# Depthwise-convolution taps on TensorE in units of 512 prompt columns, and both layer norms behind the last unit

## The chip, the cores and the metric

The kernel runs on one core of a Trainium2 chip (TensorE is PE, VectorE is DVE, ScalarE is ACT, GpSimd is POOL, SyncE is SP). The metric is the time of one execution on the device, in microseconds (us). The kernel before takes 1607.35 us, the median of three runs (1606.72 to 1612.57).

## What is computed

One inference step of a decoder of two layers, each a token mixer and a SwiGLU feed-forward, for 512 prompt tokens and 64 sample tokens (8 sequences of 8) with a model width of 1024. The first layer's mixer is a causal convolution module, and the change is inside it; the second layer's is stick-breaking attention over a paged cache. All data are fp32; a large product is made of three products of rounded parts.

```python
def conformer_conv(h, prefix, w_pw1, b_pw1, w_dw, b_dw, ln_g, ln_b, w_pw2, b_pw2):
    u = h @ w_pw1 + b_pw1
    a, gate = jnp.split(u, 2, axis=-1)
    u = a * jax.nn.sigmoid(gate)
    u_ext = jnp.concatenate([prefix.astype(u.dtype), u], axis=1)
    c = lax.conv_general_dilated(u_ext, w_dw[:, None, :], ..., feature_group_count=D_MODEL) + b_dw
    c = jax.nn.silu(layernorm(c, ln_g, ln_b))
    return c @ w_pw2 + b_pw2, u_ext[:, -CONV_STATE:]
```

The convolution has 31 taps for each of the 1024 channels, and the layer norm is over the channels of each token.

## The kernel before, in words

Channels lie on the partitions, in 8 tiles `t` of 128; the 576 tokens (512 of the prompt, 64 of the samples) are columns, in two halves `h` of 288 columns (`HALF`). The first half holds 288 prompt tokens; the second the other 224 and the 64 sample tokens.

The whole convolution stage is one graph of operations (`conv_graph`). Each operation names its engine, an estimated cost, and what it reads and writes by name; `run_ops` plays the graph through, always gives a free engine the ready operation with the longest remaining path, and so fixes the order of the instructions on each engine. On the chip every engine follows its order and waits for its data.

The stages are:

1. The first projection (`gemm`, line 580): for each `t` two products of 48 matmuls, whose results become a gate on ACT and a product on DVE (`glu_gate`, `glu_up`). DVE also does all 31 taps of the sample columns (`sample_mul`, `sample_sum`, `sample_close`, lines 661 to 679, in two pieces of 16 and 15 taps) and the last three of the 31 taps of the prompt columns (`dve_taps`, line 649). POOL and PE write out the convolution state (`state`), through two `flat` buffers.
2. The taps on PE: 28 of the 31 taps of the prompt columns. A unit is one half of the tokens of one channel tile, 16 units in all (first all tiles of half 0, then all of half 1; loop at line 864). DVE builds the unit's 28 diagonals of 32x32 (`diag`, line 615). `taps` (line 621) issues 112 matmuls of 32x32, each on one of the array's 16 places: partitions 32i of the input by a quarter 32j of the output, where the four `j` take four different taps. The trace has two records for each of these fp32 matmuls. The unit fills four PSUM banks, one for each `i`; ACT and DVE copy two each to SBUF (`tap_copy`, line 633), four matmuls add up the four quarters (`tap_sum`, line 636), and DVE adds that to its own taps (`tap_add`, line 646).
3. The layer norm of a half: `ln_first` (line 789) gets the mean by PE (`ln_mean_pe`, from a sum over six tiles that POOL made and the last two tiles), subtracts it on DVE and squares on ACT. For half 0 POOL adds the squares of the tiles and one set of token sums on PE finishes them; for half 1 PE does a set for every tile (`token_sums`, line 698). `ln_second` (line 814) takes the variance, the power on POOL, a broadcast on PE (`ln_bc`), the multiplication on DVE, silu and the rounded high part on ACT, and the low part on DVE. The norm of half 0 is put into the graph at units 8 and 11 and so runs beside the taps of half 1; the norm of half 1 comes behind the last unit, beside the second projection of half 0.
4. The second projection (`pw2`, line 833): six channel tiles of half 0, then two of half 1, 24 matmuls each; the rest belongs to the feed-forward's own graph (`ffn`, line 914), which begins with `mix_mm` for the tiles left.

PSUM has eight banks, in two sets of four. `take(s)` deals the banks of set `s` out in turn; unit `n` uses set `n % 2`. The squares have four buffers (`sq4`), dealt out in turn in program order.

Of the kernel before, what the change touches and what calls it, by code (L numbers as in the profile page):

```python
# [16 lines left out]
P = 128  # L17
D = 1024
# [43 lines left out]
def hybrid_step_kernel(  # L62
# [494 lines left out]
    with phase:  # L557
# [15 lines left out]
        csum, rstd = rbc, sacc  # L573
# [3 lines left out]

        NP = (HALF, TP - HALF)

# [53 lines left out]
        def tap_copy(c, i, b, n):  # L633
            (nc.scalar.copy, nc.vector.tensor_copy)[i % 2](cps[c][:, i, 0:n], banks[b][:, 0:n])

        def tap_sum(c, b, n):
            for i in range(4):
                r = slice(32 * i, 32 * i + 32)
                nc.tensor.matmul(
                    banks[b][r, 0:n], ident4, cps[c][:, i, 0:n], start=True, stop=True, tile_position=(0, 32 * i)  # L640
                )

        def c_part(t, h):
            return c_sb[:, t, h * HALF : h * HALF + NP[h]]

        def tap_add(t, h, b):
            nc.vector.tensor_add(c_part(t, h), c_part(t, h), banks[b][:, 0 : NP[h]])

        def dve_taps(t, h):
            c = c_part(t, h)  # L650
            for k in range(PET, W):
                u = ups[t][:, h * HALF + k : h * HALF + k + NP[h]]
# [5 lines left out]
        spr = cv.tile([P, 16, TS], F32, name="spr")  # L658
        reds = [cv.tile([P, TS], F32, name=f"red{r}") for r in range(2)]

        def sample_mul(t, r):
            k0, k1 = ((0, 16), (16, W))[r]
            u0 = us[:, t, k0, 0:1]
            win = bass.AP(tensor=us.tensor, offset=u0.offset, ap=[u0.ap[0], [NB, k1 - k0], [1, TS]])
            nc.vector.tensor_mul(
                spr[:, 0 : k1 - k0, :], win,
                vec[:, t, R_DW + k0 : R_DW + k1, None].to_broadcast([P, k1 - k0, TS]),
            )

        def sample_sum(r):  # L670
            nc.vector.tensor_reduce(
                reds[r], spr[:, 0 : 16 - r, :].rearrange("p k c -> p c k"), axis=mybir.AxisListType.X, op=ALU.add
            )

        def sample_close(t):
            nc.vector.scalar_tensor_tensor(
# [81 lines left out]
        def conv_graph():  # L758
# [13 lines left out]
            def state(t):  # L772
                f, b = ring("flat", 2), take(t % 2)
# [6 lines left out]
            def reduce_(n):  # L780
                h, t = divmod(n, NT)
                c, b = n % 2, take(n % 2)
                do("P", 0.55, [f"cp{c}_{i}" for i in range(4)], [f"b{b}"], tap_sum, c, b, NP[h])
                do("D", 0.34, [f"b{b}"] + [f"cs{t}"] * h, [f"c{t}_{h}"], tap_add, t, h, b)
                if 0 < t < SUMS:
                    cs = csum[:, HS[h]]
                    do("G", 0.76, [f"c{t}_{h}", f"c0_{h}"], [f"sum{h}"], add, cs, c_sb[:, 0, HS[h]] if t == 1 else cs, c_sb[:, t, HS[h]])

            def ln_first(h, s):
# [8 lines left out]
                qs = rstd[:, HS[h]]  # L798
                if h:
                    b = take(s)  # L800
                    do("D", 0.1, [], [f"b{b}"], nc.vector.memset, banks[b][:, 0:3], 0.0)
                for t in range(NT):
                    if t == 0 and h == 0:
                        do("A", 0.34, [f"c{t}_{h}"], ["qs"], ln_square, qs, t, h)
                        continue
# [8 lines left out]
            def ln_second(h, s, b=None):  # L814
                if h == 0:
                    b = take(s)
                    do("D", 0.1, [], [f"b{b}"], nc.vector.memset, banks[b][:, 0:3], 0.0)
                    do("P", 0.5, ["qs"], [f"b{b}"], token_sums, h, rstd[:, HS[h]], b, True, True)
# [5 lines left out]
                if h == 0:  # L824
                    do("A", 0.34, [name], ["qs"], nc.scalar.copy, rstd[:, HS[h]], m)
                    m, name = rstd[:, HS[h]], "qs"
# [15 lines left out]
            for t in range(NT):  # L842
# [12 lines left out]
                for r in range(2):  # L855
                    do("D", 1.1, [f"u{t}_1"], ["spr"], sample_mul, t, r)
                    do("D", 1.13, ["spr"], [f"red{r}"], sample_sum, r)
                do("D", 0.2, ["red0", "red1"], [f"cs{t}"], sample_close, t)
# [4 lines left out]
            stats = None  # L863
            for n in range(2 * NT):
                h, t = divmod(n, NT)
                d, c = ring("dg", 2), n % 2
                do("D", 1.1, [], [f"dg{d}"], diag, t, d)
                bs = [take(n % 2) for _ in range(4)]
                for m0, m1 in ((0, 4), (4, PET // 4)):
                    do(  # L870
                        "P", 0.6 * (m1 - m0), [f"dg{d}", f"u{t}_0"] + [f"u{t}_1"] * h, [f"b{b}" for b in bs],
                        taps, t, h, d, bs, m0, m1,
                    )
                do("D", 0.4 * (W - PET), [f"u{t}_0"] + [f"u{t}_1"] * h, [f"c{t}_{h}"], dve_taps, t, h)
                for i, b in enumerate(bs):
                    do("AD"[i % 2], 0.36, [f"b{b}"], [f"cp{c}_{i}"], tap_copy, c, i, b, NP[h])
                if n:
                    reduce_(n - 1)
# [1170 lines left out]
```

## Time and profile before

| | |
|---|---|
| median of three runs | 1607.35 us (1606.72 to 1612.57) |
| the profiled execution | 1609.35 us, of which its span from the first to the last instruction is 1607.6 us |
| PE busy | 1510.4 us, 94% |
| DVE, ACT, POOL busy | 1248.0 us (78%), 782.3 us (49%), 407.2 us (25%) |
| first projection until | 133.9 us |
| taps on PE | 133.9 to 240.4 us |
| second projection in the convolution's graph | 241.2 to 279.4 us |

The profile is of one execution, and its times count from its first instruction. A busy engine executes an instruction; PE's matmuls overlap, so that their durations add up to more than the time they take, and starts have to be compared. "issue" names idle time for which the profile shows no other engine or transfer to wait for. PEclk is the granted share of TensorE's clock.

### The profile page before, as it was taken

What the parts mean: (1) busy time and instruction counts of PE and PEld (TensorE: products, weight loads), DVE (VectorE), ACT (ScalarE), POOL (GpSimd) and SP (SyncE); (2) the same over time, 40 slices, a digit from 0 to 9 for tenths busy, and PEclk for the clock granted to TensorE, in tenths of its full rate; (3) what the DMA queues carried; (4) which work ended last, traced back from release to release, by engine and by line L of the source; (5) the groups of instructions that cost most, each with busy time, mean ns of one, the idle gap of its engine ahead of it and who ended that gap; (6) DMA issues with size and microseconds to landing.
All of it is one profiled execution on the core that took longest, in us unless ns stands there. A gap on an engine that the chain in (4) does not pass through costs nothing. (4 is left out here: it accounts for less than half of the span.)

```text
span 1607.6 us, 35925 instructions
## 1 busy us (share of the span) xinstructions
PE 1510.4 (94%) x14371; PEld 1352.6 (84%) x14371; DVE 1248.0 (78%) x2155; ACT 782.3 (49%) x1665; POOL 407.2 (25%) x410
## 2 busy tenths in 40 slices
PE   7999989899999999999999988999998999999997
PEld 7996559889999999987988875555797999999997
DVE  5998544699989999982689985555459998999884
ACT  5223123355546545552667664444435554654553
POOL 3110211333323322350244450000132322332210
PEclk9999998999999999999999989999999999999999
DMA  6233001023222233233321227999612222232231
GB/s 184 76 88 87 4 5 38 29 80 92 93 92 89 85 103 93 70 89 95 91 68 43 73 81 293 407 406 398 217 37 66 92 93 94 90 93 93 92 101 64
DMA packets 152047, 180.23 MB, mean 112 GB/s; under 512 B 6106, under 2 KB 130530, under 8 KB 151864
## 3 DMA queue, kind: packets, MB, share of 16 engines
q1 hardware_dynamic: 151448, 176.36, 33.2%
q8 instruction: 113, 1.85, 0.5%
q10 hardware_dynamic: 432, 1.57, 0.3%
q14 instruction: 54, 0.44, 0.1%
HBM read 170.45 MB, written 8.18 MB: 111 GB/s over the span
## 5 line engine op out<-in xcount | busy, mean ns | idle before, releaser
L953 DVE TENSOR_TENSOR wlo<-fs,whi 128x512 fp32r<-128x512 f32 (+1 forms) x256 | 233.5, 913 | 26.8 <-ACT whi L135 18.8
L1095 PE MATMUL fb<-ahi,whi 128*128 128x288 f32 x704 | 210.7, 299 | 14.2 <-ACT ft L135 9.4
L135 ACT CAST whi<-fs 128x512 fp32r<-128x512 f32 (+1 forms) x256 | 157.1, 614 | 134.9 <-PE fb L1095 115.6
L1095 PE MATMUL fb<-xe,whi 128*128 128x288 f32 x1056 | 216.1, 297 | 0.1
L1095 PE MATMUL fb<-alo,whi 128*128 128x288 f32 x704 | 207.7, 295 | 7.9 <-DVE alo L953 7.9
L1095 PE MATMUL fb<-ahi,wlo 128*128 128x288 f32 x704 | 211.1, 300 | 2.3 <-DVE wlo L953 2.3
L1095 PEld LDWEIGHTS fb<-xe,whi 128*128 128x128 f32 x1056 | 170.4, 189 | 0.5 <-issue 0.3
L1095 PE MATMUL fb<-xe,wlo 128*128 128x288 f32 x528 | 159.1, 301 | 2.7 <-DVE wlo L953 2.6
L1095 PEld LDWEIGHTS fb<-ahi,whi 128*128 128x128 f32 x704 | 133.3, 189 | 17.9 <-ACT ft L135 12.4
L1095 PEld LDWEIGHTS fb<-alo,whi 128*128 128x128 f32 x704 | 134.4, 191 | 8.8 <-DVE alo L953 8.8
L1095 PEld LDWEIGHTS fb<-ahi,wlo 128*128 128x128 f32 x704 | 133.2, 189 | 5.0 <-DVE wlo L953 5.0
L953 DVE TENSOR_TENSOR wlo<-wraw,whi 128x512 fp32r<-128x512 f32 (+1 forms) x160 | 124.0, 782 | 5.7 <-ACT whi L135 5.2
L135 ACT CAST whi<-wraw 128x512 fp32r<-128x512 f32 (+1 forms) x160 | 98.0, 613 | 51.8 <-PE fb L1095 46.0
L1095 PEld LDWEIGHTS fb<-xe,wlo 128*128 128x128 f32 x528 | 99.6, 189 | 7.5 <-DVE wlo L953 7.1
L135 POOL TENSOR_TENSOR fs<-wraw 128x512 f32<-128x512 f32 (+1 forms) x32 | 47.1, 1473 | 210.5 <-DVE wlo L953 210.5
L223 ACT CAST whi<-wraw 128x1024 fp32r<-128x1024 f32 (+1 forms) x43 | 44.9, 1044 | 110.7 <-PE cb L585 48.3
L135 POOL TENSOR_TENSOR fs<-wraw,fs 128x512 f32<-128x512 f32 (+1 forms) x64 | 86.0, 1343 | 50.5 <-DVE wlo L953 44.2
L135 POOL TENSOR_TENSOR fs<-fr 128x512 f32<-128x512 f32 (+1 forms) x32 | 43.7, 1364 | 208.3 <-DVE wlo L953 208.3
L1095 PE MATMUL fb<-he,whi 128*128 128x288 f32 x456 | 93.0, 297 | 2.1 <-DVE x L135 2.0
L628 PE MATMUL cb<-up,dg 32*32 32x288 f32 (+1 forms) x3584 | 80.6, 385 | 13.8 <-issue 13.5
L1095 PE MATMUL fb<-bhi,whi 128*128 128x288 f32 x304 | 90.3, 297 | 2.1 <-DVE x L135 2.1
L1095 PE MATMUL fb<-bhi,wlo 128*128 128x288 f32 x304 | 90.1, 296 | 0.0
(375 smaller groups left out, 4078.1 us busy)
## 6 DMA issues: line engine op xcount, KB each, us to landing
kr<-in_cache_k_dram SPq DMA_DIRECT2D x64, 512.0 KB
vr<-in_cache_v_dram SPq DMA_DIRECT2D x64, 512.0 KB
wraw<-in_ffn_w_up_dram SPq DMA_DIRECT2D x44, 512.0 KB
wraw<-in_cv_w_pw_dram SPq DMA_DIRECT2D x24, 512.0 KB
wraw<-in_ffn_w_down_dram SPq DMA_DIRECT2D x24, 512.0 KB
wraw<-in_sb_w_qkv_dram SPq DMA_DIRECT2D x23, 512.0 KB
fr<-in_ffn_w_gate_dram SPq DMA_DIRECT2D x22, 512.0 KB
wraw<-in_ffn_w_gate_dram SPq DMA_DIRECT2D x22, 512.0 KB
```

What stands on the lines that cost most here:

```text
L135: ops[i][3](*(a() if callable(a) else a for a in ops[i][4]))
L223: nc.scalar.copy(hi[:, :n], raw[:, :n])
L628: nc.tensor.matmul(banks[bs[i]][rj, 0:n], dgs[d][ri, k, :], ups[t][ri, h * HALF + k : h * HALF + k + n], start=(m == 0), stop=(k >= PET - ...
L953: nc.vector.tensor_sub(dst, a, b.bitcast(F32))
L1095: nc.tensor.matmul(banks[b][:, :HALF], w[:, k, :], r[:, k, :], start=(first and k == 0 and j == 0), stop=(k == nk - 1 and j == 2), skip_gr ...
```

## The change

A unit of the taps is now all 512 prompt columns of one channel tile: eight units in place of sixteen, each with the same 112 matmuls, four copies, four summing matmuls and one add, on 512 columns. `cps` grows with it, and one `flat` buffer goes; the sample taps are done in three pieces of 10, 10 and 11 with a third small sum, added at the end. DVE's own three taps and its add go over 512 columns. The layer norms of both halves now come behind the last unit: the two `ln_first` one after the other in the graph, each in the way that only half 1 had (means used from PSUM, squares to PE's token sums for every tile), then both `ln_second`. The first two tiles of the second projection of half 0 are given to the list in steps of one `k`, and its part of half 1 takes bank set 1.

```diff
-        cps = [cv.tile([P, 4, HALF], F32, name=f"cp{i}") for i in range(2)]
-        flats = [cv.tile([P, TS + PRE], F32, name=f"flat{i}") for i in range(2)]
+        cps = [cv.tile([P, 4, TP], F32, name=f"cp{i}") for i in range(2)]
+        flats = [cv.tile([P, TS + PRE], F32, name=f"flat{i}") for i in range(1)]
...
-        def taps(t, h, d, bs, m0, m1):
-            n = NP[h]
+        def taps(t, d, bs, m0, m1):
...
-                            banks[bs[i]][rj, 0:n], dgs[d][ri, k, :], ups[t][ri, h * HALF + k : h * HALF + k + n],
+                            banks[bs[i]][rj, :], dgs[d][ri, k, :], ups[t][ri, k : k + TP],
                             start=(m == 0), stop=(k >= PET - 4), tile_position=(32 * i, 32 * j),
...
-            k0, k1 = ((0, 16), (16, W))[r]
+            k0, k1 = ((0, 10), (10, 20), (20, W))[r]
...
         def sample_close(t):
+            nc.vector.tensor_add(reds[0], reds[0], reds[2])
...
-            def reduce_(n):
-                h, t = divmod(n, NT)
-                c, b = n % 2, take(n % 2)
-                do("P", 0.55, [f"cp{c}_{i}" for i in range(4)], [f"b{b}"], tap_sum, c, b, NP[h])
-                do("D", 0.34, [f"b{b}"] + [f"cs{t}"] * h, [f"c{t}_{h}"], tap_add, t, h, b)
...
+            def reduce_(t):
+                c, b = t % 2, take(t % 2)
+                both = [f"c{t}_{h}" for h in range(2)]
+                do("P", 0.95, [f"cp{c}_{i}" for i in range(4)], [f"b{b}"], tap_sum, c, b)
+                do("D", 0.6, [f"b{b}", f"cs{t}"], both, tap_add, t, b)
...
             def ln_first(h, s):
...
-                if h == 0:
-                    do("A", 0.34, [name], [f"sum{h}"], nc.scalar.copy, csum[:, HS[h]], m)
-                    m, name = csum[:, HS[h]], f"sum{h}"
...
-                    if h == 0:
-                        do("G", 0.76, [f"sq{i}"], ["qs"], add, qs, qs, sq4[i])
-                    else:
-                        do("P", 0.5, [f"sq{i}"], [f"b{b}"], token_sums, h, sq4[i], b, t == 0, t == NT - 1)
+                    do("P", 0.5, [f"sq{i}"], [f"b{b}"], token_sums, h, sq4[i], b, t == 0, t == NT - 1)
...
-            for n in range(2 * NT):
-                h, t = divmod(n, NT)
-                d, c = ring("dg", 2), n % 2
+            for t in range(NT):
+                d, c, both = ring("dg", 2), t % 2, [f"u{t}_0", f"u{t}_1"]
                 do("D", 1.1, [], [f"dg{d}"], diag, t, d)
...
-                if n == NT:
-                    ln_first(0, 1)
-                if n == NT + 3:
-                    ln_second(0, 0)
-            reduce_(2 * NT - 1)
-            b = ln_first(1, 1)
-            ln_second(1, 1, b)
+                    do("AD"[i % 2], 0.55, [f"b{b}"], [f"cp{c}_{i}"], tap_copy, c, i, b)
+                if t:
+                    reduce_(t - 1)
+            reduce_(NT - 1)
+            first = [ln_first(h, h) for h in range(2)]
+            for h in range(2):
+                ln_second(h, h, first[h])
             for t in range(6):
-                pw2((t,), 0, 0)
-            pw2((0, 1), 1, 0, 1)
+                pw2((t,), 0, 0, 1 if t < 2 else NT)
+            pw2((0, 1), 1, 1, 1)
```

## Rows read from the trace of the kernel before

**Rows 1.** The page, part 1: busy us, share of the span, instructions.

```profile
PE 1510.4 (94%) x14371; PEld 1352.6 (84%) x14371; DVE 1248.0 (78%) x2155; ACT 782.3 (49%) x1665; POOL 407.2 (25%) x410
```

**Rows 2.** Stretches: length, busy by engine (PE, PEld, DVE, ACT, POOL), PEclk, DMA share, GB/s.

```profile
40.00:133.90 93.90, 91.86 (x690) 90.93 (x689) 87.75 (x113) 21.33 (x35) 10.98 (x25) 1.00 0.28 81
133.90:188.70 54.80, 49.11 (x1865) 29.40 (x1867) 32.88 (x52) 13.31 (x27) 5.70 (x7) 1.00 0.18 48
188.70:241.20 52.50, 43.94 (x1864) 29.35 (x1863) 28.48 (x56) 15.72 (x42) 11.80 (x13) 0.99 0.02 5
...
276.40:300.00 23.60, 23.60 (x180) 23.45 (x179) 10.09 (x18) 7.13 (x18) 11.86 (x12) 1.00 0.25 81
```

**Rows 3.** Groups by shape, PE, 133.9 to 241.2: busy, mean ns | idle before.

```profile
L628 PE MATMUL cb<-up,dg 32*32 32x288 f32 x1792 | 43.7, 411 | 5.7 <-issue 5.6
L628 PE MATMUL cb<-up,dg 32*32 32x224 f32 x1792 | 36.9, 358 | 8.1 <-issue 7.9 <-DVE c_sb L647 0.2
```

**Rows 4.** Timeline of PE: start, length of the run, instructions [idle before].

```profile
174.74 1.30 PE L639 MATMUL cb<-cp,ident 128*32 128x288 f32 x16
175.97 8.60 PE L628 MATMUL cb<-up,dg 32*32 32x288 f32 x362
...
192.78 5.71 PE L628 MATMUL cb<-up,dg 32*32 32x224 f32 x276
...
206.59 2.53 PE L628 MATMUL cb<-up,dg 32*32 32x224 f32 x128 [0.84 <-issue]
210.32 2.58 PE L628 MATMUL cb<-up,dg 32*32 32x224 f32 x124 [1.20 <-issue]
...
239.19 1.22 PE L628 MATMUL cb<-up,dg 32*32 32x224 f32 x37 [1.42 <-issue]
...
241.24 0.61 PE L744 MATMUL cb<-bhi,ahi 128*128 128x288 f32 x1
...
279.38 0.29 PE L320 MATMUL fb<-bhi,ahi 128*128 128x288 f32 x1
```

**Rows 5.** Waits, 133.9 to 241.2: us in total, times, longest.

```profile
PE cb L628 <- issue: 13.5, 15, 1.8
```

**Rows 6.** DMA queues, 133.9 to 241.2: packets, MB, share of 16 engines.

```profile
q8 instruction: 29, 0.48, 1.9%
```

**Rows 7.** Groups by shape of ACT and DVE, 136 to 241.2: tap copies.

```profile
L634 ACT COPY cp<-cb 128x288 f32<-128x288 f32 x16 | 5.9, 400 | 30.9 <-PE cb L628 17.2 <-issue 13.7
...
L634 DVE COPY cp<-cb 128x288 f32<-128x288 f32 x16 | 6.8, 453 | 21.6 <-PE cb L628 20.2 <-ACT cp L634 1.2
```

**Rows 8.** Timelines of the engines: the layer norm of the second half.

```profile
254.09 6.92 PE L702 MATMUL cb<-over_d,lsq 128*128 128x1 f32 x48
...
256.89 0.44 ACT L695 ACTIVATE lsq<-c_sb 128x288 f32<-128x288 f32 x1 [0.24 <-PE cb L702]
...
261.28 0.87 POOL L711 TENSOR_TENSOR rtok<-ln,mhalf 128x3 f32<-128x3 f32 x1 [30.93 <-DVE ln L708]
...
265.62 0.56 PE L717 MATMUL cb<-ident,rtok 96*128 96x96 f32 x3
...
266.28 2.28 DVE L723 TENSOR_TENSOR c_sb<-c_sb,cb 128x288 f32<-128x288 f32 x6
...
266.77 1.15 ACT L727 ACTIVATE c_sb<-c_sb,vec 128x288 f32<-128x288 f32 x2 [9.44 <-DVE c_sb L723]
...
268.48 0.82 DVE L733 TENSOR_TENSOR blo<-c_sb,bhi 128x288 fp32r<-128x288 f32 x2
...
268.49 1.14 ACT L727 ACTIVATE c_sb<-c_sb,vec 128x288 f32<-128x288 f32 x2
```

**Rows 9.** Stretches, as rows 2, around the token sums.

```profile
257.00:258.00 1.00, 1.00 (x9) 0.97 (x8) 0.00 (x0) 0.33 (x1) 0.00 (x0) 0.61 0.00 0
...
263.00:264.00 1.00, 1.00 (x6) 1.00 (x6) 0.00 (x0) 0.00 (x0) 0.00 (x0) 0.50 0.00 0
```

**Rows 10.** Waits of the load queue, 150 to 300 us: total, times, longest.

```profile
SPq L1083 <- DVE blo L733: 120.4, 1, 120.4
```

More of the change, by code (lines that the diff above doesn't have):

```diff
@@ L628, in taps, with tap_copy, tap_sum, tap_add @@
                         nc.tensor.matmul(
-                            banks[bs[i]][rj, 0:n], dgs[d][ri, k, :], ups[t][ri, h * HALF + k : h * HALF + k + n],
+                            banks[bs[i]][rj, :], dgs[d][ri, k, :], ups[t][ri, k : k + TP],
                             start=(m == 0), stop=(k >= PET - 4), tile_position=(32 * i, 32 * j),
                         )
-        def tap_copy(c, i, b, n):
-            (nc.scalar.copy, nc.vector.tensor_copy)[i % 2](cps[c][:, i, 0:n], banks[b][:, 0:n])
-        def tap_sum(c, b, n):
+        def tap_copy(c, i, b):
+            (nc.scalar.copy, nc.vector.tensor_copy)[i % 2](cps[c][:, i, :], banks[b])
+        def tap_sum(c, b):
             for i in range(4):
                 r = slice(32 * i, 32 * i + 32)
[L639 to L650, printed above, removed]
+                nc.tensor.matmul(banks[b][r, :], ident4, cps[c][:, i, :], start=True, stop=True, tile_position=(0, 32 * i))
+        def tap_add(t, b):
+            nc.vector.tensor_add(c_sb[:, t, 0:TP], c_sb[:, t, 0:TP], banks[b])
+        def dve_taps(t):
+            c = c_sb[:, t, 0:TP]
             for k in range(PET, W):
-                u = ups[t][:, h * HALF + k : h * HALF + k + NP[h]]
+                u = ups[t][:, k : k + TP]
                 if k == PET:
@@ L656, in dve_taps @@
                     nc.vector.scalar_tensor_tensor(c, u, col(R_DW + k, t), c, ALU.mult, ALU.add)
-        spr = cv.tile([P, 16, TS], F32, name="spr")
-        reds = [cv.tile([P, TS], F32, name=f"red{r}") for r in range(2)]
+        spr = cv.tile([P, 11, TS], F32, name="spr")
+        reds = [cv.tile([P, TS], F32, name=f"red{r}") for r in range(3)]
         def sample_mul(t, r):
-            k0, k1 = ((0, 16), (16, W))[r]
+            k0, k1 = ((0, 10), (10, 20), (20, W))[r]
             u0 = us[:, t, k0, 0:1]
@@ L772, in state @@
             def state(t):
-                f, b = ring("flat", 2), take(t % 2)
+                f, b = ring("flat", 1), take(t % 2)
                 do("G", 0.6, [f"u{t}_1"], [f"flat{f}"], state_pool, t, f)
@@ L854, in conv_graph @@
                 state(t)
[L855 to L858, printed above, removed]
+                for r in range(3):
+                    do("D", 0.75, [f"u{t}_1"], ["spr"], sample_mul, t, r)
+                    do("D", 0.78, ["spr"], [f"red{r}"], sample_sum, r)
+                do("D", 0.35, ["red1", "red2"], [f"cs{t}", "red0"], sample_close, t)
             split(2 * NT + 1)
@@ L862, in conv_graph @@
                 split(c)
-            stats = None
-            for n in range(2 * NT):
-                h, t = divmod(n, NT)
-                d, c = ring("dg", 2), n % 2
+            for t in range(NT):
+                d, c, both = ring("dg", 2), t % 2, [f"u{t}_0", f"u{t}_1"]
                 do("D", 1.1, [], [f"dg{d}"], diag, t, d)
-                bs = [take(n % 2) for _ in range(4)]
+                bs = [take(t % 2) for _ in range(4)]
                 for m0, m1 in ((0, 4), (4, PET // 4)):
[L870 to L874, printed above, removed]
-                for i, b in enumerate(bs):
-                    do("AD"[i % 2], 0.36, [f"b{b}"], [f"cp{c}_{i}"], tap_copy, c, i, b, NP[h])
-                if n:
-                    reduce_(n - 1)
-                if n == NT:
-                    ln_first(0, 1)
-                if n == NT + 3:
-                    ln_second(0, 0)
-            reduce_(2 * NT - 1)
-            b = ln_first(1, 1)
-            ln_second(1, 1, b)
+                    do("P", 0.88 * (m1 - m0), [f"dg{d}", *both], [f"b{b}" for b in bs], taps, t, d, bs, m0, m1)
+                do("D", 0.6 * (W - PET), both, [f"c{t}_0", f"c{t}_1"], dve_taps, t)
+                for i, b in enumerate(bs):
+                    do("AD"[i % 2], 0.55, [f"b{b}"], [f"cp{c}_{i}"], tap_copy, c, i, b)
[3 more added lines that the diff above has]
+            first = [ln_first(h, h) for h in range(2)]
+            for h in range(2):
+                ln_second(h, h, first[h])
             for t in range(6):
-                pw2((t,), 0, 0)
-            pw2((0, 1), 1, 0, 1)
+                pw2((t,), 0, 0, 1 if t < 2 else NT)
+            pw2((0, 1), 1, 1, 1)
             run_ops()
```

29 lines of the change are left out of this document (8 added, 21 removed).

## The prediction, written before the change was run

> **What bounds the kernel now.** The page's first part comes first: PE is busy for 94% of the span [rows 1]. So the question for any edit is which PE time it takes away or lays open. The table by stretches then splits the convolution: products of the first projection until 133.9 us, taps from 133.9 to 241.2 us, then the second projection with the second half's layer norm inside it [rows 2]. In the tap stretches PE is busy 49.1 of 54.8 and 43.9 of 52.5 us while DVE, ACT and POOL are far below, so PE works alone there and what it wastes is on the path.
>
> It wastes two things. The groups of PE by shape show 1792 tap records of 288 columns and 1792 of 224: 16 units of 224 [rows 3]. The spacing inside an unbroken run (its length, less one record, over the number less one) is (8.60 - 0.41)/361 = 22.7 ns at 288 columns and (5.71 - 0.36)/275 = 19.5 ns at 224 [rows 3, 4]. That is 0.05 ns for a further column, so a large part of a record costs the same whatever its width. And there are pauses: in the timeline runs of exactly 128 records end in idle time "issue" [rows 4], 13.5 us of PE in 15 waits [rows 5]. The instruction queue moved 29 packets in these 107.3 us [rows 6], one each 3.70 us. Some 3730 matmul records with as many weight loads stand against them [rows 2], 257 instructions a packet, 128 of them matmuls. 128 records of 224 columns take 2.5 us, far less than 3.70, and a pause follows; the start of one such run to the next is 3.73 us [rows 4]. I read the stage as held by how fast instructions arrive.
>
> **The taps.** Sixteen units become eight: 1792 records of 512 columns instead of 3584. One record: 22.7 + 224 x 0.05 = 33.9 ns, a unit 224 x 33.9 = 7.6 us. Bounds: the shortest spacing, (2.53 - 0.36)/127 = 17.1 ns in a run of 128 at 224 columns [rows 3, 4], extended by the same slope to 31.5 ns, a unit 7.1 us; in proportion to columns, 22.7 x 512/288 = 40.4 ns, a unit 9.0 us. I take 33.9: the long runs contain whatever slows a run a little, and two widths fix a line.
>
> A packet's 128 records now last 128 x 33.9 = 4.34 us, more than the 3.70 us at which packets came, so I cost the pauses at nothing; if they stay, one of 13.5/15 = 0.9 us follows each of some 14.6 packets, 13 us. The Trainium skill (Runtime: NRT & Kernel Launch, Instruction fetch mechanics) holds that the next block is fetched while the present one runs and that crossing a block is mostly hidden. The rows differ: pauses stand at every 128th matmul. By the page they have another cause and need not go; that is the first rival.
>
> The tap sums: two together hold the next taps back for 1.23 us at 288 columns (174.74 to 175.97) [rows 4], 0.6 us each. One of 512 columns I take at 1.0 us (between 0.7, if records count, and 1.1, in proportion); seven lie before the last tap's end, the eighth behind it.
>
> Stage: start 133.9 + 8 x 7.6 + 7 x 1.0 + 0.7 for a state transpose and bank waits = **202.4 us** for the last tap's end, where it is now 239.19 + 1.22 = 240.41 [rows 4]. That is 38.0 us less.
>
> **Beside the taps, at nothing.** DVE builds eight diagonals fewer and runs its own three taps in 24 instructions of 512 columns instead of 48 shorter ones, which saves fixed costs; its sample work goes from two pieces to three with one small add, which adds some. The columns stay the same, so in the first stretch its 87.8 of 93.9 us [rows 2] stays about even. Were DVE pushed there, PE would wait for gate products; each unit has a whole product of slack, so I bound it at 1 us either way. One flat buffer instead of two only makes POOL's copy wait for a transpose of the tile before, a product earlier. The copies out of PSUM (400 ns for 288 columns on ACT, 453 on DVE [rows 7]) grow, in proportion to 0.71 and 0.81 us at most, four per unit on two engines, hidden under 7.6 us. No DMA is moved by itself.
>
> **The layer norm is laid open.** Now the first half's norm lies under the second half's taps. After the change nothing stands behind the taps but the norms. From the last tap (e): two copies on each engine, e + 0.9; the sum's last matmuls, e + 1.5; the add of 512 columns (taken like a copy, 453 ns at 288 [rows 7]) from e + 1.65 to 2.35; the mean product's last operand, e + 3.2, and behind it on PE the other half's mean (1.4 us by the list's own cost), e + 4.7. Subtractions and squares feed PE's token sums: 48 records in 6.92 us for one half [rows 8]. The change does both halves that way, where now one half is added on POOL and summed once. The four square buffers are dealt out in program order, so the second half's squares follow the first's, and the list puts the broadcast behind the token sums whose remaining path is longer, nearly all of them. So I count 16 tiles' sums before the first broadcast. What is a tile's price? The last square (256.89) reuses the fourth's buffer and starts as that one's sums end: (256.89 - 254.09)/4 = 0.7 us a tile. Then the granted clock fell from full to half (2.4 to 1.2 GHz), three microseconds into the token sums, and the last four tiles took (261.0 - 256.9)/4 = 1.0 us each [rows 8, 9]. After the change PE has been half idle since e, so I take 1.0: 16 us (bounds 11 and 17), until e + 20.8. Variance, power (0.87 us on POOL, of the first half hidden) and broadcast (0.56 us at full clock), e + 21.6. The first multiplication starts at 266.28, the low half of the first split at 268.48 [rows 8]; the first matmul, which needs the high half only, can start 2.2 us behind the broadcast. **The second projection starts at e + 23.8**; now it starts 241.24 - 240.41 = 0.8 us behind the last tap [rows 4]. That costs 23.0 us.
>
> **The second projection gets shorter.** Now it runs from 241.24 to 279.38 [rows 4], 38.1 us, though its 192 matmuls (8 tile halves of 24) at 23.6/180 = 0.13 us, as in the undisturbed stretch behind it [rows 2], are some 25.5: the token sums (6.9), means, broadcast, tap sum and half clock stand inside. After the change these are done before. PE then has 25.6 us, about 1.6 us for half clock at the start (it was still half three microseconds after the token sums [rows 9]), and ACT feeds one channel tile of one half (silu and split) in (268.49 - 266.77)/2 = 0.86 us [rows 8] against 0.8 us of PE work on it, which costs about 1 us: 28.2 us. That returns 9.9 us.
>
> **Sum:** -38.0 + 23.0 - 9.9 = -24.9 us. Behind it the feed-forward order is unchanged and PE is its first stretch's limit; its first weight load waits for the last split of the second half [rows 10], which comes 15 us ahead of the projection's end instead of 6, so nothing is late there. The profiled execution took 1609.35 us (span 1607.6), 2 us above the median of 1607.35; against the median the sum is 1582.5 us.
>
> **The rivals.** *Pauses stay* (13 us): 1595.5 us. For it: 29 packets and pauses agree in number, but a queue that is only late by a constant would stay so. Against it: longer unbroken runs exist at 288 columns (362 records). *Packs don't overlap:* with one record's duration grown to 411 + 224 x (411 - 358)/64 = 597 ns [rows 3] and the next sixteen waiting for these, 41 ns a record, a unit 9.2 us, +12.8 us, 1595 us. Against it: at 288 the same would be over 25 ns, and rows show 22.7. The Trainium skill (TensorE: Matmul & The Clock Gate, Measured speedup vs the span model) gives a pack's span as one matmul's duration plus 4 ns for each further tile, which at 288 columns would be 29 ns a record; the trace disagrees, packs overlap. *Both norms before any product:* the list lets ACT finish both halves first, 14 us more ahead of the projection and little regained: 1596.5 us. *Taken back later:* the feed-forward starts no earlier because its weights do not come; its load queue is idle until then [rows 10], so they should: about 1605 us. *Slower:* fewer 32x32 tiles run at once at 512 columns. Now 411/22.7 = 18 records are in flight (durations hold the pipeline too); with 12, 597/12 = 50 ns a record, 28.9 us more than forecast, 1611.4 us. It decides from 33.9 + 24.9/1.792 = 47.8 ns. Nothing in the rows shows a limit at either width. That the change is void can be excluded: half the tap instructions are gone.
>
> **Chances.** Forecast 0.63, pauses 0.14, packs 0.07, both norms 0.06, taken back 0.06, slower 0.04. A measurement tells about 0.5% (8 us) from no change: 1599.3 us is the border. The first four lie under it, with 0.02 off for two of them together: faster 0.88, same 0.08, slower 0.04. The range: short records and full-clock token sums (-4, -5 us), with shorter tap sums (-2 us), give 1571 us, the three rivals near 1596 with some of a second one 1599 us. It holds more than eight in ten by my cases; I leave the ends because the tap price rests on two widths.
>
> **What would show it.** Taps x1792 of 512 columns spaced near 34 ns, hardly any "issue" waits in 133 to 202 us, some 15 instruction packets there; last tap near 202 us; an idle or half-clock PE for 23 us, token sums of both halves in it; first projection matmul near 226 us; the first feed-forward matmul near 254 us and the same stage lengths after it. Spacings above 40 ns, a pause per 128 records, or a projection starting later than 30 us behind the taps prove the steps wrong.

## The result and the profile after

The changed kernel takes 1579.38 us, the median of four runs (1579.24 to 1581.0); the kernel before took 1607.81 us beside it (four runs, 1606.72 to 1612.57). The ratio is 0.9819, with a 95% interval of 0.9804 to 0.9833, so 28.4 us less; 24.9 us less were forecast. The profiled executions stand 1609.35 to 1581.0 us, spans 1607.6 to 1579.2 us. The stages, from the timelines of PE:

| us from the span's start | before | predicted | after |
|---|---|---|---|
| first tap | 133.88 | 133.9 | 133.08 |
| last tap's end (e) | 240.41 | 202.4 | 199.79 |
| first matmul of the second projection | 241.24 | 226.2 | 223.59 |
| first matmul of the feed-forward | 279.38 | 254.4 | 251.99 |
| end of the span | 1607.6 | | 1579.2 |

The taps end 40.6 us earlier. Of that 23 us are given back before the projection starts, 9.7 us come back inside the projection, and the feed-forward starts 27.4 us earlier. Behind it only one more microsecond is won, which single executions differ by.

The page of the changed kernel, part 1 (busy us, share of the span, instructions), answers to [rows 1]:

```profile
PE 1497.1 (95%) x12557; PEld 1344.9 (85%) x12557; DVE 1234.3 (78%) x2123; ACT 781.8 (50%) x1647; POOL 397.0 (25%) x403
```

PE's busy time fell by 13.3 us only, against 28.4 us of the span: half of the gain is idle time of PE. The stretches show where it stood (as in [rows 2]: length, busy by engine, PEclk, DMA share, GB/s):

```profile
133.00:200.00 67.00, 67.00 (x1847) 40.74 (x1849) 36.67 (x51) 16.59 (x27) 8.86 (x12) 1.00 0.13 38
...
215.00:220.00 5.00, 5.00 (x27) 4.88 (x28) 0.00 (x0) 0.89 (x2) 0.00 (x0) 0.50 0.01 2
```

In the tap stage PE is now busy for all of 67 us, where it was busy for 93 of 107 us [rows 2]. From 215 to 220 us it is "busy" too, but almost alone, at half clock, while DVE does nothing and ACT 0.89 us: these are the token sums. The timeline of PE, beside [rows 4] and [rows 8]:

```profile
138.13 11.07 PE L624 MATMUL cb<-up,dg 32*32 32x512 f32 x320
149.14 1.97 PE L635 MATMUL cb<-cp,ident 128*32 128x512 f32 x16
151.04 15.06 PE L624 MATMUL cb<-up,dg 32*32 32x512 f32 x448
...
184.73 15.06 PE L624 MATMUL cb<-up,dg 32*32 32x512 f32 x448
199.72 1.92 PE L635 MATMUL cb<-cp,ident 128*32 128x512 f32 x16
...
204.59 16.03 PE L694 MATMUL cb<-over_d,lsq 128*128 128x1 f32 x96
220.54 0.93 PE L709 MATMUL cb<-ident,rtok 128*128 128x128 f32 x3
...
223.59 0.61 PE L736 MATMUL cb<-bhi,whi 128*128 128x288 f32 x1 [0.86 <-ACT bhi L722]
...
251.99 0.40 PE L320 MATMUL fb<-bhi,ahi 128*128 128x288 f32 x1
```

Runs of 448 taps, two whole units, now stand without a break where runs of 128 ended in "issue" before. Two sums follow each pair of units. Then 96 records of token sums (both halves, 16 tiles) fill 16 us, and only behind the last of them comes the broadcast of the first half. The group by shape (133 to 252 us, which holds all taps) and the instruction queue (133.9 to 200 us), against [rows 3] and [rows 6]:

```profile
L624 PE MATMUL cb<-up,dg 32*32 32x512 f32 x1792 | 61.1, 597 | 0.0
```

```profile
q8 instruction: 14, 0.23, 1.5%
```

The 1792 records have no idle time ahead of them at all; before, 13.5 us of "issue" stood there [rows 5]. 14 packets were fetched in place of 29.

Last, the token sums. The squares on ACT show their pace, since each takes the buffer of the square four before it (timelines of ACT, then stretches as above):

```profile
206.70 0.45 ACT L687 ACTIVATE lsq<-c_sb 128x288 f32<-128x288 f32 x1 [0.24 <-PE cb L694]
207.39 0.45 ACT L687 ACTIVATE lsq<-c_sb 128x288 f32<-128x288 f32 x1 [0.24 <-PE cb L694]
...
210.50 0.44 ACT L687 ACTIVATE lsq<-c_sb 128x288 f32<-128x288 f32 x1 [0.69 <-PE cb L694]
211.63 0.44 ACT L687 ACTIVATE lsq<-c_sb 128x288 f32<-128x288 f32 x1 [0.69 <-PE cb L694]
```

```profile
206.00:207.00 1.00, 1.00 (x10) 0.97 (x10) 1.00 (x4) 0.74 (x2) 0.00 (x0) 1.00 0.00 0
207.00:208.00 1.00, 1.00 (x10) 0.96 (x9) 1.00 (x4) 0.59 (x2) 0.00 (x0) 0.79 0.00 0
208.00:209.00 1.00, 1.00 (x6) 0.98 (x6) 1.00 (x4) 0.44 (x1) 0.00 (x0) 0.50 0.00 0
```

A tile's sums take 0.69 us at the full 2.4 GHz and 1.13 us at 1.2 GHz; the granted clock falls to half inside 207 to 208 us, three microseconds into the sums, as in [rows 9].

### The profile page after: what moved, and what is told of

Same layout as the page of the kernel before. It is cut to its first block, busy times and chain, and to the rows that moved or that the text cites. A ratio compares the mean times of both kernels' runs of the same rounds, so it can differ in the third digit from the quotient of the medians.

```text
span 1579.2 us, 32209 instructions
## 1 busy us (share of the span) xinstructions
PE 1497.1 (95%) x12557; PEld 1344.9 (85%) x12557; DVE 1234.3 (78%) x2123; ACT 781.8 (50%) x1647; POOL 397.0 (25%) x403
## 3 DMA queue, kind: packets, MB, share of 16 engines
q1 hardware_dynamic: 151448, 176.36, 33.9%
## 5 line engine op out<-in xcount | busy, mean ns | idle before, releaser
L1062 PE MATMUL fb<-blo,whi 128*128 128x288 f32 x304 | 89.0, 293 | 0.4 <-DVE blo L920 0.4
```

Of the source, the lines that this page charges most:

```text
L1062: nc.tensor.matmul(banks[b][:, :HALF], w[:, k, :], r[:, k, :], start=(first and k == 0 and j == 0), stop=(k == nk - 1 and j == 2), skip_gr ...
```

## The experiments

### Fewer columns in a tap: is it the arrival of instructions that made the pauses?

Three kernels keep the changed kernel's instructions, one for one, and only let the taps on PE (with their copies, sums and adds) work on the first N of the 512 prompt columns; PE's taps of the other columns are left out.

```diff
-   banks[bs[i]][rj, :], dgs[d][ri, k, :], ups[t][ri, k : k + TP],
+   banks[bs[i]][rj, 0:N], dgs[d][ri, k, :], ups[t][ri, k : k + N],
...
-   (nc.scalar.copy, nc.vector.tensor_copy)[i % 2](cps[c][:, i, :], banks[b])
+   (nc.scalar.copy, nc.vector.tensor_copy)[i % 2](cps[c][:, i, 0:N], banks[b][:, 0:N])
```

N = 128:

> The changed kernel with the taps, their copies, sums and adds on the first 128 of the 512 prompt columns only: the other 384 columns keep DVE's three taps alone, so a part of the convolution is left out. The number of PE instructions stays. If PE is held by the arrival of its instructions (one packet of 128 matmul records with their weight loads each 3.7 us, as in the kernel before), 1792 records still need 14 packets: 52 us for the taps, last tap near 186 us, and a pause of 1.5 us or more behind every 128 records, which by themselves last 1.9 us (14.7 ns each by the line of the prediction). If a pause is a fixed 0.9 us at each 128 records: 26 + 13 + 3 us for sums, last tap near 175 us. If pauses belong to a unit (waits for its banks), 26 + 7 + 3 us, last tap near 169 us.

N = 256:

> As the one on 128 columns, with 256 columns: the second half of each unit is left out. Arrival of instructions: the same 52 us as with 128 columns, last tap near 187 us, pauses near 1.0 us (128 records last 2.7 us by 21 ns each). A fixed pause of 0.9 us: 38 + 13 + 5 us, last tap near 189 us, that is 14 us later than with 128 columns. The two runs tell it: same end means arrival, 14 us apart means columns.

N = 384, run after the other two:

> The changed kernel with PE's taps, their copies, sums and adds on the first 384 of the 512 prompt columns (the taps of the other 128 columns are left out of PE's share). Theory (a matmul record takes as long as its columns need, but 128 of them can't come faster than once in 3.45 us, as at 128 and 256 columns): a straight line through 22.7 ns at 288 and 32.4 ns at 512 columns gives 26.9 ns, 3.44 us for 128, which is just the rate at which they come; so the last tap ends at about the same 187 us as at 128 and 256 columns, and the issue waits shrink from 4.5 us (256 columns) to under 2 us. Rival (no common rate; the time follows the columns): between 256 columns (186.2) and 512 columns (199.8), the last tap ends in the middle, at 193 us.

Measured, one run each: 1570.77 us (N = 128), 1568.38 us (256), 1571.9 us (384), beside 1581.0 us of the changed kernel's own profiled run. From the first tap to the last tap's end it is 56.0, 54.1 and 58.6 us, against 66.7 us at 512. The issue waits are 9.3, 4.5, 0.3 and 0 us; those at 128 and 256 columns as the view of waits has them (us in total, times, longest):

```profile
PE cb L624 <- issue: 9.3, 10, 2.3
PE cb L624 <- issue: 4.5, 8, 0.9
```

The timelines of PE, first at 128 columns:

```profile
133.09 2.32 PE L624 MATMUL cb<-up,dg 32*32 32x128 f32 x128
...
138.00 2.11 PE L624 MATMUL cb<-up,dg 32*32 32x128 f32 x128 [0.22 <-issue]
142.00 1.53 PE L624 MATMUL cb<-up,dg 32*32 32x128 f32 x102 [1.89 <-issue]
...
169.20 2.81 PE L624 MATMUL cb<-up,dg 32*32 32x128 f32 x128 [0.92 <-issue]
```

at 256 columns:

```profile
166.33 2.75 PE L624 MATMUL cb<-up,dg 32*32 32x256 f32 x128 [0.61 <-issue]
169.79 2.80 PE L624 MATMUL cb<-up,dg 32*32 32x256 f32 x128 [0.71 <-issue]
```

and at 384:

```profile
160.44 1.83 PE L624 MATMUL cb<-up,dg 32*32 32x384 f32 x54 [0.34 <-issue]
...
164.01 12.17 PE L624 MATMUL cb<-up,dg 32*32 32x384 f32 x448
...
177.60 12.94 PE L624 MATMUL cb<-up,dg 32*32 32x384 f32 x448
```

At 256 columns the pauses are back, behind runs of exactly 128, though the units are the same eight: so it is not the number of units that took them away, but the width. The starts of such runs lie 3.46 us apart (169.79 - 166.33), of which 2.8 us are work and about 0.65 us a pause. At 224 columns, in the kernel before, it was 2.5 us of work and a start 3.73 us [rows 4] or 3.45 us (231.73 to 235.18) after the last: less work, longer pause. At 384 columns 128 records take 3.3 to 3.6 us ((12.17 - 0.49)/447 x 128 in the run at 164.01), and one pause of 0.34 us is left; at 512 they take 4.14 us and none is. A fixed pause per packet would have stayed at 384 and 512. So the theory holds: while no other transfers run, 128 matmuls come once in 3.45 to 3.73 us, and a run that is shorter waits for the difference. Longer runs stand unbroken at a faster pace for a while (362 records at 288 columns, 2.9 us for 128 [rows 4]; 448 at 384 columns, 3.3 us). They begin behind a tap sum, during which packets can come in ahead; this reason is argued, not tested.

The interval is longer where weights are being loaded at the same time. In the kernel before (timeline of PE, then a stretch as above):

```profile
154.67 3.02 PE L628 MATMUL cb<-up,dg 32*32 32x288 f32 x128 [1.04 <-issue]
159.49 1.51 PE L628 MATMUL cb<-up,dg 32*32 32x288 f32 x54 [1.80 <-issue]
```

```profile
154.60:157.70 3.10, 3.02 (x128) 1.93 (x128) 0.95 (x3) 1.57 (x3) 0.00 (x0) 1.00 1.03 279
```

Here the DMA engines were busy (279 GB/s), and the next 128 came after 4.82 us; with a DMA share of 0.02 it was 3.73 us (206.59 to 210.32 [rows 4]) and 3.45 us (231.73 to 235.18). At 128 columns the longest such interval, 5.1 us from 152.64 to 157.74 us, also lies beside weights being loaded. That the loads are the cause was not tested: no run moves them.

The kernel at 128 columns alone proves less than it was meant to. Its last tap ends at 189.1 us, nearer the theory's 186 than the 175 and 169 us of the others, but not for the theory's reason alone. Its runs are no shorter than those at 256 columns, with TensorE at half clock (stretches, as above):

```profile
140.00:144.00 4.00, 2.11 (x117) 1.40 (x109) 4.00 (x6) 0.29 (x1) 0.00 (x0) 0.93 0.59 174
144.00:148.00 4.00, 0.89 (x8) 0.31 (x6) 3.96 (x7) 1.08 (x3) 0.00 (x0) 0.50 0.41 113
...
184.00:188.00 4.00, 3.38 (x182) 2.63 (x161) 0.64 (x3) 0.53 (x2) 0.00 (x0) 0.50 0.02 4
```

PE had just waited 1.89 us for instructions (until 142.00); the clock fell to 0.50 near 143.5 us, PE then waited 2.3 us for a copy on DVE, and the clock stayed there to the last tap. At 256 columns PE waited 2.6 us for the same copy and the clock fell too (0.50 from 148 to 150 us), but it was full again from 151 us on; why it did not rise at 128 columns is not shown. While it was full, a record took (2.32 - 0.38)/127 = 15.3 ns. So at 128 columns, 224 [rows 4] and 256 the same picture holds, but the nearly equal ends of 128 and 256 columns (189.1 and 186.2 us, expected 186 and 187) are in part the clock's.

At 384 columns neither number of the expectation came out: the last tap ends at 190.5 us, between 187 and 193. The record was priced rightly (26.9 ns; measured 26.1 in the run at 164.01, 27.8 in the last), and the pauses went. What the expectation forgot is the tap sums: at 384 columns nothing is being waited for, and each pair lies open (162.19 to 164.01, 1.8 us). At 256 columns a pair takes 1.3 us (160.21 to 161.54), but the 256 records from 158.88 to 166.33, with a pair among them, took 7.45 us, only 0.5 us more than two intervals of 3.46 us: the next instructions come in meanwhile.

### The norms moved, without the units

> The kernel before with the second part of the change alone: sixteen units of half the tokens stay, both layer norms come behind the last unit as in the changed kernel. My theory: the last tap comes at 239.5 us, the second projection starts 23.8 us later and runs 28.4 us, so the feed-forward starts at 291.7 instead of 279.4 us: 1620 us, 12 us slower than the kernel before, and the units by themselves are worth about 40 us. Rival: what the norms lay open is given back in full by the shorter projection, 1609 us, and the units are worth the 28 us of the whole change.

```diff
-                if n == NT:
-                    ln_first(0, 1)
-                if n == NT + 3:
-                    ln_second(0, 0)
             reduce_(2 * NT - 1)
-            b = ln_first(1, 1)
-            ln_second(1, 1, b)
+            first = [ln_first(h, h) for h in range(2)]
+            for h in range(2):
+                ln_second(h, h, first[h])
```

(with `ln_first`, `ln_second` and the order of the second projection as in the change). Measured: 1617.86 us (1617.01 to 1618.48), a ratio of 1.0059 with an interval of 1.0042 to 1.0076, so 9.7 us more than before. The theory is right, its 12 us somewhat too much. The other part then follows by difference: with both norms behind the last tap in either case, eight units in place of sixteen (with the sample taps in three pieces, which go with them) are worth 1617.9 - 1579.4 = 38.5 us by the medians and 237.1 - 199.8 = 37.3 us by the last taps; the prediction's tap term was 38.0. Its timeline of PE shows the same token sums laid open:

```profile
236.45 0.64 PE L628 MATMUL cb<-up,dg 32*32 32x224 f32 x22 [1.12 <-issue]
...
242.77 12.37 PE L702 MATMUL cb<-over_d,lsq 128*128 128x1 f32 x84
...
258.12 0.61 PE L744 MATMUL cb<-bhi,whi 128*128 128x288 f32 x1 [0.86 <-ACT bhi L730]
```

Here the projection starts 21.0 us behind the last tap, not 23.8: 12 of the 96 sum records are done ahead of the second mean, at 239.83 us.

### The token sums taken off PE

> The changed kernel, but the squares of the first half are added up on DVE and those of the second on POOL, and PE makes one set of token sums for each half in place of eight. If the 16 us of token sums on PE at half clock are what lies between the taps and the projection, the projection starts about 14.5 us behind the last tap instead of 23.8 and the kernel takes 1570 us (9 us less than the changed one). Rival: the chain of subtractions, squares and adds on DVE, ACT and POOL sets that time, with POOL's adds stretching DVE's subtractions (753 instead of 454 ns in the kernel before): projection 20 us behind the taps, 1575 to 1579 us.

```diff
-                for t in range(NT):
-                    i = ring("sq", 4)
+                qs = sacc[:, HS[h]]
+                do("A", 0.34, [f"c0_{h}"], [f"qs{h}"], ln_square, qs, 0, h)
+                for t in range(1, NT):
+                    i = 2 * h + ring(f"sq{h}", 2)
                     do("A", 0.34, [f"c{t}_{h}"], [f"sq{i}"], ln_square, sq4[i], t, h)
-                    do("P", 0.5, [f"sq{i}"], [f"b{b}"], token_sums, h, sq4[i], b, t == 0, t == NT - 1)
+                    e, cost = (nc.vector, 0.37) if h == 0 else (nc.gpsimd, 0.76)
+                    do("DG"[h], cost, [f"sq{i}"], [f"qs{h}"], e.tensor_add, qs, qs, sq4[i])
+                do("P", 0.5, [f"qs{h}"], [f"b{b}"], token_sums, h, qs, b, True, True)
```

Measured: 1576.0 us (1575.76 to 1576.71), ratio 0.9802 (0.9788 to 0.9816). The rival's time, not the theory's. PE and DVE:

```profile
214.03 2.34 PE L694 MATMUL cb<-over_d,sacc 128*128 128x1 f32 x12 [8.82 <-DVE sacc L135]
...
219.41 0.61 PE L736 MATMUL cb<-bhi,whi 128*128 128x288 f32 x1 [0.92 <-ACT bhi L722]
```

PE's 16 us of sums are 2.3 us now, but it stands idle for 8.8 us until DVE has done the subtractions of both halves and the additions of one, near 214 us. The projection starts 19.2 us behind the last tap (219.41 - 200.26) instead of 23.8. One bound was taken away, and DVE's own work stood 4.6 us behind it.

### The first half's norm first

> The changed kernel with the squares added off PE (first half on DVE, second on POOL, one set of token sums each), and the second half's subtractions held until the first half's squares are added. In the run that only moved the sums, the projection started 19.2 us behind the last tap because DVE did both halves' subtractions in between. If that order was the rest of the price, the first half's token sums come near 210 us instead of 214, the projection starts near 215 us, and the kernel takes 1571 us. Rival: PE then waits for the second half instead, whose token sums stand early in PE's order, and the gain is lost: 1575 to 1577 us.

```diff
-                    do("D", 0.37, [name], [f"c{t}_{h}"], ln_sub, t, h, m)
+                    do("D", 0.37, [name] + ["qs0"] * h, [f"c{t}_{h}"], ln_sub, t, h, m)
```

(over the kernel of the section before; the buffers of the squares are one ring of four again). Measured: 1575.42 us (1573.66 to 1577.31), ratio 0.9793 (0.9775 to 0.9812); again the rival's time. DVE and POOL:

```profile
208.63 3.00 DVE L684 TENSOR_TENSOR c_sb<-c_sb,cb 128x288 f32<-128x288 f32 x8
211.54 0.16 DVE L700 TENSOR_SCALAR ln<-cb 128x3 f32<-128x3 f32 x1
```

```profile
210.05 2.54 POOL L135 TENSOR_TENSOR sacc<-sacc,lsq 128x288 f32<-128x288 f32 x3 [22.23 <-ACT lsq L687]
212.55 0.87 POOL L703 TENSOR_TENSOR rtok<-ln,mhalf 128x3 f32<-128x3 f32 x1
```

The first half's token sums are done at 210.0 us, but its variance stands behind all eight subtractions of the second half on DVE, and its power behind three additions of the second half on POOL. What the second half was held back for, it took away one step later. On PE:

```profile
216.44 0.61 PE L736 MATMUL cb<-bhi,whi 128*128 128x288 f32 x1 [2.05 <-ACT bhi L722]
...
217.81 1.04 PE L694 MATMUL cb<-over_d,sacc 128*128 128x1 f32 x6
...
221.11 0.87 PE L709 MATMUL cb<-ident,rtok 96*128 96x96 f32 x3
```

The first projection matmul comes 17.3 us behind the last tap, 1.9 us better than in the kernel of the section before. But the projection now takes 31.1 us instead of 28.7, so that the feed-forward starts 48.4 us behind the last tap instead of 47.9: the gain is lost, as the rival said, though PE works on the second half there and does not wait for it. Part of the 2.4 us is the second half's own token sums and broadcast, which now stand inside the projection (1.8 us); the rest is the next question.

### Keeping PE busy

> As the kernel with the first half first, and 44 matmuls of 256 columns without use on PE behind the second mean, into a bank that is free then, to see what the granted clock costs. If half clock in the token sums, broadcasts and the first 3 us of the projection costs what the trace shows (about 3 us), this kernel is 2 to 3 us faster than the one without them. Rival: the clock has fallen again by the time of the projection, or the matmuls delay the token sums: 0 to 1 us faster, or slower.

```diff
+        def filler(b):
+            w = parts[2 * NT][0]
+            for i in range(44):
+                nc.tensor.matmul(banks[b][:, 0:256], w[:, i % 8, :], w[:, 0:2, :].rearrange("p k c -> p (k c)"), start=True, stop=True)
...
+                if h:
+                    bf = take(s)
+                    do("P", 0.3, [name, *w_names(2 * NT)], [f"b{bf}"], filler, bf)
```

Measured: 1576.45 us (1575.14 to 1577.91), ratio 0.9801 (0.9783 to 0.9819): no gain. PE and the stretches:

```profile
202.89 5.64 PE L748 MATMUL cb<-whi 128*128 128x256 f32 x44
...
212.65 0.93 PE L709 MATMUL cb<-ident,rtok 128*128 128x128 f32 x3 [3.63 <-POOL rtok L703]
```

```profile
205.00:210.00 5.00, 4.02 (x36) 3.92 (x34) 4.79 (x14) 3.04 (x8) 0.76 (x1) 1.00 0.00 0
210.00:213.00 3.00, 0.35 (x2) 0.29 (x2) 0.88 (x4) 1.51 (x4) 2.84 (x5) 0.68 0.01 3
...
216.00:220.00 4.00, 3.89 (x17) 3.63 (x17) 2.28 (x7) 3.51 (x9) 1.01 (x1) 0.50 0.00 0
```

The useless matmuls end at 208.5 us and the first half's token sums at 209.0. The clock is full to 210 us, where it was half by then in the kernel before this one; it is 0.68 in the mean of 210 to 213 us, in which PE is nearly idle again, and half from there. The projection starts at 1.2 GHz all the same, at 215.62 us, 17.4 us behind the last tap as without the useless matmuls. A filling that runs to the very start of the projection was not tried.

### The second half put into the gaps

> The kernel of e5, but half 1's first five subtractions are held until half 0's variance is taken on DVE, and its last three until the third channel tile of half 0 is split, so that nothing of half 1 stands in DVE's or POOL's order ahead of half 0's variance, power and multiplications. Theory (the start of the second projection is set by the latency of half 0's norm alone, and in e5 its variance waited 1.5 us behind half 1's subtractions and its power 0.9 us behind POOL's adds): variance near 210.0, power done near 211.1, broadcast done near 212.1, first projection matmul near 214.2 instead of 216.4, first feed-forward matmul near 245.3 instead of 247.5, and 1573.2 us. Rival (a projection that starts earlier only runs longer at half clock, as e6's did, or ACT, which now has half 1's squares between the silus, feeds it too slowly): the first projection matmul is earlier, the first feed-forward matmul stays within 0.7 us of 247.5, and 1575 to 1576 us.

```diff
-                    do("D", 0.37, [name] + ["qs0"] * h, [f"c{t}_{h}"], ln_sub, t, h, m)
+                    do("D", 0.37, [name] + ["bl2_0" if t > 4 else "var0"] * h, [f"c{t}_{h}"], ln_sub, t, h, m)
...
-            first = [ln_first(h, h) for h in range(2)]
             for h in range(2):
-                ln_second(h, h, first[h])
+                ln_power(h, ln_first(h, h))
+                ln_second(h, h)
```

(`ln_power` is the variance and the power, cut out of `ln_second`). Measured: 1576.58 us (1571.1 to 1578.06), ratio 0.979 (0.9775 to 0.9806). PE and ACT:

```profile
211.48 0.93 PE L709 MATMUL cb<-ident,rtok 128*128 128x128 f32 x3 [1.20 <-POOL rtok L703]
215.64 0.61 PE L736 MATMUL cb<-bhi,whi 128*128 128x288 f32 x1 [3.23 <-ACT bhi L722]
```

```profile
213.47 0.42 ACT L687 ACTIVATE lsq<-c_sb 128x288 f32<-128x288 f32 x1
213.81 0.41 ACT L722 CAST bhi<-c_sb 128x288 fp32r<-128x288 f32 x1
...
215.18 0.41 ACT L722 CAST bhi<-c_sb 128x288 fp32r<-128x288 f32 x1
```

The broadcast comes 2.0 us earlier than in the kernel with the first half first (211.48 for 213.47), as the theory said, yet the first projection matmul only 0.8 us earlier: ACT has squares of the second half among the first silus and high parts, and the matmul follows the second high part, which ends at 215.59. And of the 0.8 us the feed-forward gets 0.5 (247.03), within the rival's 0.7 us; the median lies 0.6 us above the rival's range and 3.4 us above the theory's, in runs from 1571.1 to 1578.06 us. The rival is nearer.

Over five of the kernels (the last tap comes at 198.2 to 200.3 us in these executions, so the times are counted from it; the matmuls at half clock are those that start before the granted clock, read in stretches of one or two microseconds, rises):

| | last tap's end | first projection matmul | first feed-forward matmul | projection matmuls at half clock | second half's sums and broadcast inside the projection |
|---|---|---|---|---|---|
| the change | 199.8 | +23.8 | +52.2 | 15 | none |
| token sums off PE | 200.3 | +19.2 | +47.9 | 15 | none |
| first half first | 199.1 | +17.3 | +48.4 | 24 | 1.8 us |
| the same with useless matmuls | 198.2 | +17.4 | +48.8 | 25 | 1.8 us |
| second half in the gaps | 199.4 | +16.2 | +47.6 | 25 | 1.8 us |

Matmuls of the projection stand 0.24 us apart at half clock and 0.13 us at full, so 9 or 10 more of them at half clock cost about 1 us. This and the second half's 1.8 us on PE are where most of the earlier starts of the last three kernels went. What makes the clock rise when it does is not shown. The first step, from the change to the sums off PE, lost almost nothing: 4.6 us at the projection, 4.3 us at the feed-forward.

### The sample taps in three pieces, alone

> The kernel before with the sample taps in three pieces alone. In the changed kernel the first tap starts at 133.1 instead of 133.9 us. If the shorter pieces on DVE let gates through earlier, the first tap starts near 133.1 us here too; if it is the taps of DVE over 512 columns, it stays at 133.9 us.

```diff
-            k0, k1 = ((0, 16), (16, W))[r]
+            k0, k1 = ((0, 10), (10, 20), (20, W))[r]
```

(in the kernel before, with `spr`, `reds` and `sample_close` to match). Measured: 1606.37 us in one run, the kernel before 1608.28. The first tap comes at 132.32 us instead of 133.88. But over all kernels here with three pieces it comes anywhere from 131.60 to 133.09 us, and with two pieces at 133.88 (before) and 131.92 (norms moved alone). The difference lies within what executions differ by; that the three pieces gain or cost anything can't be told.

## Why the prediction was right

**The taps, -38.0.** Right: -40.6 by the timeline, -37.3 to -38.5 by the kernels with and without the units. From 133.08 to 199.79 us are 66.7 us. Three pairs of sums take 1.90, 1.85 and 1.86 us of it and a state transpose 0.24, which leaves 60.9 us, 7.6 us a unit: the price taken, between bounds of 7.1 and 9.0. That it came out to a tenth is luck. In the runs of 448, records are (15.06 - 0.60)/447 = 32.3 ns apart, and 32.5 ns over all five runs, not 33.9, which is 2.4 us less over the stage; the ends of the five runs, which the sum behind them doesn't cover and the prediction didn't count, take 2.5 us. At other widths the same straight line gives 14.7 ns at 128 columns (22.7 - 160 x 0.05), where 15.3 were measured, and 27.5 at 384, where it was 26.1 and 27.8 in the runs shown.

The 2.6 us by which the last tap came too early are in the smaller terms. Seven sums at 1.0 us were counted before the last tap; six came, in pairs, at 0.94 us: 1.4 us less. For a transpose and bank waits 0.7 us were put down, 0.24 were there. And the stage began 0.8 us earlier, which is within what executions differ by.

**The pauses, at nothing.** Right, and this was the step with most against it (13 us). The rival's price was read wrongly: packets and pauses do not agree in number, and a pause does not stand at every 128th matmul; 15 waits [rows 5] stand against 29 packets [rows 6]. Kept at the rate of the kernel before, 14.6 packets would have meant 13.5 x 14.6/29 = 6.8 us. The Trainium skill (Runtime: NRT & Kernel Launch, Instruction fetch mechanics) has the next block of instructions fetched while the present one runs, and the crossing mostly hidden. The runs at 256 and 512 columns show when that holds here: with 4.1 us of work in a packet's 128 matmuls the crossing is hidden, with 2.8 us it isn't, and about 0.65 us stand open between two runs of 128. The 3.70 us of the prediction is a mean over the whole stage; the interval is 3.45 us at its shortest, and 4.8 us where weights were being loaded.

**The norm laid open, +23.0.** Right to a tenth: the projection starts 23.8 us behind the last tap, as predicted, and each step in it lies where it was put. The token sums begin at e + 4.8 (4.7 predicted) and last 15.95 us (16). The tile price of 1.0 us was meant as the price at half clock, but it came from a stretch that began at full clock. In truth there are two prices, 0.69 us until the clock falls and 1.13 us after it; PE began the sums at full clock and fell to half three microseconds into them, so that their mean over 16 tiles is 1.0. That the two meet there is luck: at half clock throughout, by an estimate from these rows, the sums would have taken 16 x 1.13 = 18 us. The list did put the first half's broadcast behind all 16 tiles' sums: its power was done at 213.8 us, and it then waited 6.7 us in PE's order.

**The projection, -9.9.** Right: 28.4 us for 28.2. 15 matmuls ran at half clock, 1.6 us as taken; the 1 us put down for ACT's feeding was there as well, but as one wait at the start, for the first low half on DVE (223.59 to 224.80 us).

**Behind it, nothing.** Right: the feed-forward starts 27.4 us earlier, the span ends 28.4 us earlier.

So the whole error, 3.5 us, is 0.8 us of the stage's start, 1.4 + 0.5 us of the sums and the allowance, and 1.0 us behind the feed-forward's start, less 0.2 us of the projection.

**The rivals.** *Pauses stay*: there were none. *Packs don't overlap*: the duration it was built on came out to the nanosecond (597 ns), but the records are 32.3 ns apart, not 41. The Trainium skill (TensorE: Matmul & The Clock Gate, Measured speedup vs the span model) gives the span of one pack as one duration and 4 ns for each further tile, which makes an estimate of (597 + 60)/16 = 41 ns here, if each pack waits for the one before it. The trace shows 32.3 ns, so packs overlap, as they did at 288 columns; 597/32.3 = 18 records are in flight at either width. *Slower* by fewer in flight falls with the same number. *Both norms before any product*: ACT did not finish both halves first; the first product came behind the first high part, at 223.59 us. *Taken back later*: it was not.

**What was left lying.** The sums on PE are 16 us of which most are at half clock. Taking them off PE, with DVE and POOL adding, gives 1575.4 to 1576.6 us in four forms, 0.9790 to 0.9802 of the kernel before, and the feed-forward starts 3.4 to 4.6 us earlier behind the last tap than in the change. All four are faster than the kernel before; against the change itself they are ahead by some 3 us in the medians, with intervals that overlap its own; among themselves the four can't be told apart. The 9 us that were hoped for first are not there, because DVE's chain stands right behind, and then the second half's own sums and broadcast and the half clock.

## What to carry to other kernels

When PE runs many short matmuls, look for runs of equal count that end in "issue", and compare the work in one run with the spacing of the instruction packets: wider instructions then win twice, once by their smaller fixed share and once by hiding the fetch. Price work that is laid open by the row of the same work at the clock that will be granted there, and count what the list puts ahead of the first instruction that matters. When one bound in a latency chain is taken away, look at what each in-order engine has queued ahead of the next step before promising its whole price.

## What was not expected of the hardware

At 128 columns the tap stage itself fell to half clock (0.50 from 144 us to its end) behind waits for instructions and, around the fall, for copies. Fewer columns so gave no shorter runs: 2.81 us for 128 records, against 2.77 us at 256 columns and full clock.

The instruction packets came slower beside the loads of weights (4.8 and 5.1 us for 128 matmuls, against 3.45 us), which no figure of the prediction had.

Useless work on PE kept the granted clock at 1.00 from 205 to 210 us, but what the projection got out of it was nothing: PE idled once more, 3.6 us ahead of the broadcast, and the projection began at half clock as before.
